# Top-2-of-8 experts on one core: four column groups for gate and up, transposes on the vector engine, a computed one-hot, another order and another end

## The chip, the cores and the metric

The kernel runs on one core of one Trainium2 chip. The metric is the device time of one execution in microseconds (us), and the number that counts is the median of the runs of one kernel. Before the change there were three runs: 1240.44, 1244.74 and 1244.99 us, so the median is 1244.74 us.

The engines are named as in the profile: PE is the matrix engine with its queue of matmuls, PEld its weight loads, DVE the vector engine, ACT the scalar engine, SP the engine that only issues DMA transfers here.

## The reference

The program is a decoder trunk of two residual layers over 256 tokens of 1024 channels, all in float32. Each layer has a token mixer (not touched here) and a channel mixer: a dense SwiGLU in layer 0, and in layer 1 eight SwiGLU experts of which every token uses two:

```
logits = tokens @ router_w                      # 256 x 8
top_val, top_idx = top_k(logits, 2)             # two experts for each token
top_w = softmax(top_val)
out[token] += top_w * ((silu(x_e @ gate[e]) * (x_e @ up[e])) @ down[e])   # for both experts of the token
x = x + out
```

`gate[e]` and `up[e]` are 1024x1792 and `down[e]` is 1792x1024: 22 MB of weights for each expert, 176 MB for the eight, which are all read once from memory in every execution.

## The kernel before, in words

**Stages.** Mixer 0, dense SwiGLU, mixer 1 and then the experts, which take the time from 794 us to the end. Within each engine the instructions run in the order in which the program writes them (`manual_schedule`): no instruction of a queue passes another. What stands between engines is waits on semaphores that the compiler sets for the data.

**Slots.** An expert has 96 places for tokens ("slots", `CAP`), in three blocks of 32 (`CG`). A one-hot matrix `oh` (token by slot, from the rank `pos` of a token within its expert, `onehot`) says which token has which slot. `gather` (L1090s) multiplies the tokens, split in two float32r halves `th` and `tl`, by the one-hot, and so makes `xe`: channels by slots, for two experts at once; each call makes half of the channels (16 matmuls of 192 columns and two copies when nothing was made ahead). The compiled program has the count `n` of tokens of each expert in a register. `rest` (L1104) puts the matmuls of the third block under `If(n > 64)`: on these inputs the third block runs for experts 0, 1, 2 and 4 and is skipped for 3, 5, 6 and 7. A second pass (`more`) for experts with over 96 tokens exists in the program and does not run.

**Weights.** Every weight tile is 128 rows by 1024 columns (512 KB), or 128 by 768 in a second gate/up round (384 KB). SP issues their transfers at L87 (`feed`), in a fixed order, 24 tiles ahead of the tile that PE uses (`RA_MOE`), into 46 places that are also used for the other big buffers (`xe`, `es`, `aT`, `ye`, `ohT`). An issue waits until its place is free. For expert e the order is: gate and up of round 0 (16 tiles), the last six down tiles of expert e-1, gate and up of round 1 (16 tiles), the first eight down tiles of e. PE consumes them in this order.

**One expert.** `gate_up` (L1114) is called twice, for 1024 and for 768 of the 1792 columns. The weights are the moving operand, the slots the stationary one, 32 columns of PE wide, so that four matmuls stand beside each other in the four column groups of PE. Two column blocks (512 or 384 columns, `BN`) by two slot blocks make the four groups: eight matmuls for a pair of gate and up tiles, and after four such pairs those of the third slot block into a bank of its own. A tile's place comes free when the third block's matmuls have read it. Then silu on ACT and products on DVE. `turn` (L1145) transposes the result on PE through two banks (`ps_et`), with one copy on ACT and one on DVE, into `aT`. `down` (L1158) multiplies by the down tiles, four matmuls of 512 columns each, and again the third block after each group of tiles. `scale` (L1177) multiplies the finished rows by the routing weights and splits them in two halves (ACT, then DVE, twice). `back` (L1188) transposes the one-hot with four PE transposes and one ACT copy. `scatter` (L1198) multiplies the transposed one-hot by the rows (16 matmuls), and DVE adds the result to `x`; for the last expert SP then stores each quarter.

**Order.** The loop of `experts` (L1214) interleaves two experts:

```
gate_up(e, 0); down(1) of e-1; scale; back of e-1; turn; [odd e: gather half]
gate_up(e, 1); down(0) of e; turn; [odd e: gather other half]; scatter of e-1
```

At e = 1 `slot_weights` (64 matmuls of two columns, L1084) stands between `down(1)` and `scale`. PE's on-chip accumulators are eight banks of 512 columns, given out in turn.

Of the kernel before, what the change touches and what calls it, by code (L numbers as in the profile page):

```python
# [31 lines left out]
O_ID, O_TU, O_TUS, O_TLS, O_ONE, O_IOTA, O_LT, O_CNT = 0, 128, 256, 384, 512, 640, 768, 832  # L32
O_SLOT = 896
N_CONST = 1152
# [9 lines left out]
BN = (512, 384)  # L44
# [4 lines left out]
class Net:  # L49
# [990 lines left out]
    def moe(self, l, out):  # L1040
# [70 lines left out]
        def group(ps, g, n):  # L1111
            return ps[g * CG:(g + 1) * CG, :n]

        def gate_up(e, i, xe, n):  # L1114
# [3 lines left out]
            if n is not None:  # L1118
                nc.vector.memset(pr[:, :w], 0.0)
            for c in range(2):  # L1120
                ws = []
                for k in range(4 * c, 4 * c + 4):
                    ws.append((self.get_raw(), self.get_raw()))
                    for m, ps in enumerate((pg, pu)):
                        for b in range(2):
                            for s in range(2):
                                mmf(group(ps, 2 * b + s, w), x(k, s), ws[-1][m][:, b * w:(b + 1) * w],  # L1127
                                    start=(k == 0), stop=(k == KD - 1))
                    self.pulse()

                def f():
                    for k in range(4 * c, 4 * c + 4):
                        for m in (1, 0):
                            for b in range(2):
                                mmf(group(pr, 2 * (1 - m) + b, w), x(k, 2), ws[k - 4 * c][m][:, b * w:(b + 1) * w],
                                    start=(k == 0), stop=(k == KD - 1))
                rest(n, f)
            a = self.u("es")
            nc.scalar.activation(a[:, :w], pg[:, :w], AF.Silu)  # L1139
            nc.vector.tensor_mul(a[:, :w], a[:, :w], pu[:, :w])  # L1140
            nc.scalar.activation(a[:64, 512:512 + w], pr[64:, :w], AF.Silu)
            nc.vector.tensor_mul(a[:64, 512:512 + w], a[:64, 512:512 + w], pr[:64, :w])
            return a

        def turn(a, i):  # L1145
            pa, pb = self.ps("et"), self.ps("et")
            at = self.u("aT")[:, :NJ[i] * CAP].rearrange("p (j s) -> p j s", s=CAP)
            n = BN[i] // P
            for c in range(n):
                nc.tensor.transpose(pa[:, c * P:(c + 1) * P], a[:, c * P:(c + 1) * P], self.ident)  # L1150
            for c in range(n):
                nc.tensor.transpose(pb[:, c * 64:(c + 1) * 64], a[:64, 512 + c * P:512 + (c + 1) * P],
                                    self.ident[:64, :64])
            nc.scalar.copy(at[:, :, :64], pa[:, :n * P].rearrange("p (j s) -> p j s", s=64))
            nc.vector.tensor_copy(at[:, :, 64:], pb[:, :n * 64].rearrange("p (j s) -> p j s", s=32))
            return at

        def down(i, at, acc, n):  # L1158
            for c0, c1 in ((0, 4), (4, NJ[i])):
                ws = []  # L1160
                for j in range(c0, c1):
                    ws.append(self.get_raw())
                    for b in range(2):
                        for s in range(2):
                            mmf(group(acc[0], 2 * b + s, 512), at[:, j, s * CG:(s + 1) * CG],  # L1165
                                ws[-1][:, b * 512:(b + 1) * 512], start=(i + j == 0), stop=(i == 1 and j == NJ[1] - 1))
                    self.pulse()

                def f():
                    for j in range(c0, c1):  # L1170
                        for b in range(2):
                            mmf(group(acc[1], 2 * b + j % 2, 512), at[:, j, 2 * CG:], ws[j - c0][:, b * 512:(b + 1) * 512],
# [15 lines left out]
        def back(oh, e):  # L1188
            pt = self.ps("ohT")
            for q in range(2):  # L1190
                for t in range(2):
                    nc.tensor.transpose(pt[:, (2 * q + t) * P:(2 * q + t + 1) * P],  # L1192
                                        self.slots(oh, t, e, q).bitcast(F32), self.ident)
            o = self.u("ohT", F32R)
            nc.scalar.copy(o[:, :512], pt)  # L1195
            return o

        def scatter(y, o, last):  # L1198
            for t in range(2):
                ps = [self.ps("sc"), self.ps("sc")]  # L1200
                for q in range(2):
                    for p in range(2):
                        for b in range(2):
                            r = slice(64 * b, 64 * (b + 1))
                            mmf(ps[b], o[r, (2 * q + t) * P:(2 * q + t + 1) * P], y[q][r, p * 512:(p + 1) * 512],  # L1205
                                start=(q + p == 0), stop=(q + p == 2))
                for b in range(2):
                    h = slice(b * 512, (b + 1) * 512)
                    x = self.x[:, t, h]
                    nc.vector.tensor_add(x, x, ps[b])  # L1210
                    if last:
                        nc.sync.dma_start(out[t * P:(t + 1) * P, h], x)

        def experts(oh, wch, skip):  # L1214
# [3 lines left out]
            acc = y = prev = None  # L1218
            for e in range(NE + 1):
                if e < NE:  # L1220
                    x = xe[e // 2]
                    n = None
                    if skip:
                        n = nc.values_load(self.cni[0:1, e:e + 1], min_val=0, max_val=T, engines=[mybir.EngineType.PE])
# [199 lines left out]
```

## Time and profile before

| | us |
|---|---|
| median of three runs | 1244.74 |
| the profiled execution, its time | 1241.17 |
| its span | 1239.3 |
| PE busy in it | 1203.8 (97%) |
| DVE busy | 640.4 (52%) |
| ACT busy | 442.1 (36%) |

The profile shows one execution. Its span is the time from the first to the last event that the hardware profiler recorded; its own time is 1.9 us longer. Busy time is the time in which an engine had an instruction in work; matmuls overlap, so a row of the timeline that holds eight matmuls gives the time from the start of the first to the end of the last. The granted clock is the share of full speed that PE had (1.00 is 2.4 GHz, 0.50 is 1.2 GHz). A DMA share of 1 means that all 16 DMA engines of the core had packets in work all the time. In the slices of the page, the moved bytes rise from some 150 to 200 GB/s in the first two thirds to over 400 GB/s in the last quarter, which is the experts.

### The profile page before, as it was taken

To read this page: it belongs to the slowest core of one execution; us is meant where nothing else is said; L and a number is where in the kernel's file an instruction comes from. 1 tells how busy PE (TensorE), PEld (TensorE's weight loads), DVE (VectorE), ACT (ScalarE), POOL (GpSimd) and SP (SyncE) were. 2 spreads that over 40 slices of the span, in tenths; PEclk is the share of its full clock that TensorE was granted. 3 is DMA by queue.
4 is the path that set the end of the run, shared out by engine and by line. 5 is a ranking of instruction groups with operands and counts; after the bars stand their busy time and mean duration, and the time that the engine had idled before them with its cause. 6 is when DMAs were issued, how large, how long until landed. Compare 5 with 4: busy or idle time off the path is not lost. (4 is left out here: it accounts for less than half of the span.)

```text
span 1239.3 us, 22611 instructions
## 1 busy us (share of the span) xinstructions
PE 1203.8 (97%) x9536; PEld 885.7 (71%) x9536; DVE 640.4 (52%) x951; ACT 442.1 (36%) x628; POOL 22.7 (2%) x24
## 2 busy tenths in 40 slices
PE   7999999999999999999999999999999999999985
PEld 5899989998899998899989999433433343343322
DVE  6799867686645555789866776510111121112112
ACT  6555555453534543556556442200101011011010
POOL 0100000000000000100000000000000000000000
PEclk9999999999999999999999999899999999999999
DMA  9545444565566564445543569599799999999995
GB/s 367 194 148 188 153 153 136 172 225 216 176 199 198 176 204 174 146 135 171 170 154 122 178 197 348 193 357 373 303 366 349 402 408 403 405 405 399 407 403 205
DMA packets 91122, 312.27 MB, mean 252 GB/s; under 512 B 10240, under 2 KB 10624, under 8 KB 91008
## 3 DMA queue, kind: packets, MB, share of 16 engines
q1 hardware_dynamic: 91008, 310.66, 69.0%
q8 instruction: 83, 1.36, 0.4%
q14 instruction: 31, 0.25, 0.1%
HBM read 309.57 MB, written 1.05 MB: 251 GB/s over the span
## 5 line engine op out<-in xcount | busy, mean ns | idle before, releaser
L100 DVE TENSOR_TENSOR wlo<-raw,whi 128x1024 fp32r<-128x1024 f32 x244 | 289.3, 1218 | 69.3 <-ACT whi L95 61.6
L95 ACT CAST whi<-raw 128x1024 fp32r<-128x1024 f32 x244 | 243.8, 1048 | 19.0 <-DMA raw<-in_w_mix_dram 5.0
L1127 PE MATMUL ps_gg<-raw,xe 128*32 128x384 f32 (+1 forms) x1024 | 121.9, 546 | 2.3 <-PEq L1108 1.4
L1127 PE MATMUL ps_gu<-raw,xe 128*32 128x384 f32 (+1 forms) x1024 | 120.9, 542 | 0.9 <-DMA raw<-in_w_gu_dram 0.4
L1140 DVE TENSOR_TENSOR es<-es,ps_gu 128x512 f32<-128x512 f32 (+1 forms) x16 | 9.9, 621 | 208.1 <-ACT es L1139 171.6
L1165 PE MATMUL ps_ye<-raw,aT 128*32 128x512 f32 x896 | 104.8, 595 | 7.3 <-DMA raw<-in_w_dn_dram 4.6
L157 PE MATMUL ps_gate<-hh,whi 128*128 128x256 f32 x384 | 111.4, 290 | 0.0
L159 PE MATMUL ps_gate<-hl,whi 128*128 128x256 f32 x384 | 108.6, 283 | 0.0
L158 PE MATMUL ps_gate<-hh,wlo 128*128 128x256 f32 x384 | 108.6, 283 | 0.0
L1139 ACT ACTIVATE es<-ps_gg 128x512 f32<-128x512 f32 (+1 forms) x16 | 8.7, 544 | 220.2 <-PE ps_gg L1127 165.9
L1165 PEld LDWEIGHTS ps_ye<-raw,aT 128*32 128x32 f32 x896 | 28.7, 109 | 78.3 <-issue 51.9
L1127 PEld LDWEIGHTS ps_gu<-raw,xe 128*32 128x32 f32 x1024 | 33.7, 110 | 66.0 <-issue 51.9
L1127 PEld LDWEIGHTS ps_gg<-raw,xe 128*32 128x32 f32 x1024 | 31.4, 110 | 64.0 <-issue 49.8
L157 PEld LDWEIGHTS ps_gate<-hh,whi 128*128 128x128 f32 x384 | 73.5, 192 | 0.5
L158 PEld LDWEIGHTS ps_gate<-hh,wlo 128*128 128x128 f32 x384 | 73.5, 191 | 0.5
L159 PEld LDWEIGHTS ps_gate<-hl,whi 128*128 128x128 f32 x384 | 73.5, 191 | 0.0
L157 PE MATMUL ps_xbc<-hh,whi 128*128 128x256 f32 x256 | 73.2, 286 | 0.0
L159 PE MATMUL ps_xbc<-hl,whi 128*128 128x256 f32 x256 | 72.4, 283 | 0.0
L158 PE MATMUL ps_xbc<-hh,wlo 128*128 128x256 f32 x256 | 72.3, 283 | 0.0
L157 PE MATMUL ps_u<-hh,whi 128*128 128x256 f32 x208 | 59.0, 283 | 0.0
L159 PE MATMUL ps_u<-hl,whi 128*128 128x256 f32 x208 | 58.9, 283 | 0.0
L158 PE MATMUL ps_u<-hh,wlo 128*128 128x256 f32 x208 | 58.9, 283 | 0.0
(333 smaller groups left out, 2496.5 us busy)
## 6 DMA issues: line engine op xcount, KB each, us to landing
raw<-in_w_mix_dram SPq DMA_DIRECT2D x178, 512.0 KB, 3.8
raw<-in_w_gu_dram SPq DMA_DIRECT2D x128, 512.0 KB, 10.0
raw<-in_w_dn_dram SPq DMA_DIRECT2D x112, 512.0 KB, 10.0
raw<-in_w_gu_dram SPq DMA_DIRECT2D x128, 384.0 KB, 7.9
raw<-in_w_ffn_dram SPq DMA_DIRECT2D x66, 512.0 KB, 4.4
gain<-in_gains_dram SPq DMA_DIRECT2D x6, 512.0 KB, 4.5
out_dram<-x_res SPq DMA_DIRECT2D x4, 256.0 KB, 3.4
x_res<-in_x_dram SPq DMA_DIRECT2D x2, 256.0 KB, 3.1
```

Source lines behind the costliest of these rows:

```text
L95: nc.scalar.copy(hi, self.raws[self.nhi])
L100: nc.vector.tensor_sub(lo, self.raws.pop(self.nlo), hi.bitcast(F32))
L157: mm(out, lh, rh, start=start, stop=False)
L158: mm(out, ll, rh, start=False, stop=False)
L159: mm(out, lh, rl, start=False, stop=stop)
L1127: mmf(group(ps, 2 * b + s, w), x(k, s), ws[-1][m][:, b * w:(b + 1) * w], start=(k == 0), stop=(k == KD - 1))
L1139: nc.scalar.activation(a[:, :w], pg[:, :w], AF.Silu)
L1140: nc.vector.tensor_mul(a[:, :w], a[:, :w], pu[:, :w])
L1165: mmf(group(acc[0], 2 * b + s, 512), at[:, j, s * CG:(s + 1) * CG], ws[-1][:, b * 512:(b + 1) * 512], start=(i + j == 0), stop=(i == 1 and ...
```

## The change

What it does, part by part:

- **Column groups.** `BN` becomes (256, 192): in `gate_up` the four column groups of PE hold four column blocks of the same slot block, and the slot blocks stand one behind the other in the columns of the accumulator. A tile of gate or up is used by eight matmuls of 256 or 192 columns in place of four of 512 or 384; the third slot block takes four for each tile in place of two of double width.
- **Transposes.** The products then have 32 slots in each group of 32 partitions, and one DVE instruction transposes them in squares of 32 by 32 into `aT`, within `gate_up`. `turn`, with its PE transposes and copies, is gone. The down weights are laid out in memory to fit the new order of rows.
- **One-hot.** `back` no longer transposes the one-hot: DVE makes two diagonal matrices of the positions (`dg`), one PE matmul with a matrix of ones spreads them over all partitions (`pb`, one matmul of 256 columns), and two DVE comparisons with the slot's own number make the transposed one-hot.
- **Order.** Both halves of the next `gather` now come before `gate_up(e, 1)`. The scattering of expert e-1 (`add_back`) comes before `down(0)`, ahead of the clearing of the accumulator `ye` on DVE. It uses four banks; the matmuls of the third slot block are under `If(n > 64)`.
- **End.** For the last expert `back` comes before the first down rows. Before the last down rows four matmuls by the identity load `x` into the four banks; the scattering adds to them, ACT and DVE copy two banks each, and each copy is followed by a store.
- The constants are rearranged to fit.

The core of the diff:

```diff
-BN = (512, 384)
+BN = (256, 192)
...
         def gate_up(e, i, xe, n):
...
-                        for b in range(2):
-                            for s in range(2):
-                                mmf(group(ps, 2 * b + s, w), x(k, s), ws[-1][m][:, b * w:(b + 1) * w],
-                                    start=(k == 0), stop=(k == KD - 1))
+                        for s in range(2):
+                            for b in range(4):
+                                mmf(group(ps, b, s * 256, w), x(k, s), ws[-1][m][:, b * w:(b + 1) * w],
+                                    start=(k + s == 0), stop=(k + s == KD))
...
+            nc.scalar.activation(a2, v(pg), AF.Silu)
+            nc.scalar.activation(a[:, 2 * w:3 * w], pr[:, :w], AF.Silu)
+            nc.vector.tensor_mul(a2, a2, v(pu))
+            nc.vector.tensor_mul(a[:, 2 * w:3 * w], a[:, 2 * w:3 * w], pr[:, 256:256 + w])
+            at = self.u("aT")
+            nc.vector.transpose(at[:, :3 * w], a[:, :3 * w])
+            return lambda j, s: at[:, s * w + j * CG:s * w + (j + 1) * CG]
-        def turn(a, i):
...
-        def back(oh, e):
-            pt = self.ps("ohT")
+        def back(e, pos):
+            dg = self.small("dg", T, F32R)
+            for t in range(2):
+                c = t * NE + e
+                nc.vector.tensor_scalar(dg[:, self.tok(t)], self.ident, pos[:, c:c + 1], None, op0=ALU.mult)
+            pb = self.ps("pb")
+            mmf(pb[:, :T], self.one_r, dg, start=True, stop=True)
+            o = self.u("ohT", F32R)
             for q in range(2):
-                for t in range(2):
-                    nc.tensor.transpose(pt[:, (2 * q + t) * P:(2 * q + t + 1) * P],
-                                        self.slots(oh, t, e, q).bitcast(F32), self.ident)
-            o = self.u("ohT", F32R)
-            nc.scalar.copy(o[:, :512], pt)
+                nc.vector.tensor_scalar(o[:, q * T:(q + 1) * T], pb[:, :T], self.c[:, O_SP + q:O_SP + q + 1], None,
+                                        op0=ALU.is_equal)
             return o
...
+        def scatter(y, o, n, ps, first):
+            def part(q, p, start=False, stop=False):
                 for t in range(2):
+                    for b in range(2):
+                        r = slice(64 * b, 64 * (b + 1))
+                        mmf(ps[t][b], o[r, (2 * q + t) * P:(2 * q + t + 1) * P], y[q][r, p * 512:(p + 1) * 512],
+                            start=start, stop=stop)
+            part(0, 0, start=first)
+            rest(n, lambda: (part(1, 0), part(1, 1)))
+            part(0, 1, stop=True)
+        def add_back(y, o, n):
+            ps = [[self.ps("sc") for _ in range(2)] for _ in range(2)]
+            scatter(y, o, n, ps, True)
+            for t in range(2):
                 for b in range(2):
+                    x = self.x[:, t, b * 512:(b + 1) * 512]
+                    nc.vector.tensor_add(x, x, ps[t][b])
...
         # the loop of experts, after
+            for e in range(NE):
+                at0 = gate_up(e, 0, x, n)
                 if e:
+                    down(1, at1, acc, n0)
                     if e == 1:
                         slot_weights(oh)
                     y = scale(e - 1, acc)
+                    o = back(e - 1, pos)
                 if e % 2 and e < NE - 1:
+                    for q in range(2):
+                        gather(oh, e // 2 + 1, xe[e // 2 + 1], q)
+                at1 = gate_up(e, 1, x, n)
+                if e:
+                    add_back(y, o, n0)
                 acc = [self.ps("ye"), self.ps("ye")]
                 if n is not None:
                     nc.vector.memset(acc[1], 0.0)
+                if e == NE - 1:
+                    o = back(e, pos)
+                down(0, at0, acc, n)
+                n0 = n
+            ps = [[self.ps("sc") for _ in range(2)] for _ in range(2)]
+            h = lambda b: slice(b * 512, (b + 1) * 512)
+            for t in range(2):
+                for b in range(2):
+                    mmf(ps[t][b], self.ident, self.x[:, t, h(b)], start=True, stop=False)
+            down(1, at1, acc, n0)
+            scatter(scale(NE - 1, acc), o, n0, ps, False)
+            for t in range(2):
+                for b in range(2):
+                    (nc.vector.tensor_copy if b else nc.scalar.copy)(self.x[:, t, h(b)], ps[t][b])
+                    nc.sync.dma_start(out[t * P:(t + 1) * P, h(b)], self.x[:, t, h(b)])
```

## Rows read from the trace of the kernel before

Times are us from the start of the span. In an order of work a row holds the start, the duration, the engine and line, what was done (result <- operands, partitions by columns) and the count.

**Rows 1.** Busy time by stage: us, engines, granted clock, DMA share, GB/s

```profile
794.00:961.00 167.00, 166.15 (x1656) 62.27 (x1652) 22.47 (x47) 15.34 (x28) 0.00 (x0) 0.99 0.87 329
961.00:1220.00 259.00, 247.49 (x2346) 92.58 (x2337) 44.58 (x80) 27.00 (x50) 0.00 (x0) 1.00 1.03 404
...
860.00:880.00 20.00, 20.00 (x172) 11.23 (x168) 4.23 (x8) 3.30 (x6) 0.00 (x0) 0.91 0.91 345
```

**Rows 2.** SyncE's waits, 794-961 us: waited for, total us, times, longest

```profile
SPq L87 <- PE ps_gr L1135: 69.7, 16, 13.3
```

**Rows 3.** Order of work, SyncE, 947 to 950 us: start, us, what was issued

```profile
948.19 2.27 SPq L87 DMA_DIRECT2D raw<-in_w_gu_dram  x5
```

**Rows 4.** Order of work, PE, the router: start, us, matmuls

```profile
773.89 0.43 PE L930 MATMUL ps_lg<-hT,wg 128*32 128x128 f32 x8
```

**Rows 5.** Groups by line and shape: count | busy us, mean ns

```profile
L848 PE MATMUL ps_pm<-win,pw 128*128 128x256 f32 x16 | 4.1, 378 | 0.0
L930 PE MATMUL ps_lg<-hT,wg 128*32 128x128 f32 x32 | 1.8, 285 | 0.0
...
L213 DVE CAST cstr<-cst 128x128 fp32r<-128x128 f32 x1 | 0.2, 218 | 0.0
```

**Rows 6.** Order of work, PE, around the end of expert 0's first round

```profile
813.94 0.66 PE L1150 MATMUL ps_et<-cst,es 128*128 128x128 f32 x4
...
815.84 0.85 PE L1127 MATMUL ps_gg<-raw,xe 128*32 128x384 f32 x8
```

**Rows 7.** Order of work, expert 1; then PE after its down rows

```profile
874.62 0.66 PE L1192 MATMUL ps_ohT<-cst,oh 128*128 128x128 f32 x4
...
875.74 1.41 DVE L1183 SCALAR_TENSOR_TENSOR ye<-ps_ye,sw,ye 128x512 fp32r<-128x512 f32 x2 [0.76 <-ACT ye L1182]
...
876.03 0.36 PE L991 MATMUL ps_ga<-oh,th 128*128 128x192 f32 x1
...
879.27 1.15 PE L1127 MATMUL ps_gg<-raw,xe 128*32 128x384 f32 x8
...
905.49 0.55 PE L1150 MATMUL ps_et<-cst,es 128*128 128x128 f32 x3
...
906.29 0.36 PE L991 MATMUL ps_ga<-oh,th 128*128 128x192 f32 x1
...
908.25 2.12 PE L1205 MATMUL ps_sc<-ye,ohT 64*128 64x512 f32 x16
```

**Rows 8.** Order of work, all engines, expert 2

```profile
938.77 0.66 PE L1192 MATMUL ps_ohT<-cst,oh 128*128 128x128 f32 x4
...
939.70 0.75 DVE L1183 SCALAR_TENSOR_TENSOR ye<-ps_ye,sw,ye 128x512 fp32r<-128x512 f32 x1 [0.19 <-ACT ye L1182]
...
940.18 0.85 PE L1127 MATMUL ps_gg<-raw,xe 128*32 128x384 f32 x8
```

**Rows 9.** SyncE's waits, 996 to 1001 us

```profile
SPq L87 <- PEq L1108: 3.7, 1, 3.7
```

**Rows 10.** The DMA view, 961-1220 us: GB/s in 40 slices, issues

```profile
GB/s 408 397 402 399 408 409 409 404 412 402 397 400 408 407 405 412 406 409 397 396 406 407 409 407 407 407 399 395 386 408 405 407 411 407 409 395 397 406 407 388
...
q8 instruction: 24, 0.39, 0.6%
...
raw<-in_w_dn_dram SPq DMA_DIRECT2D x70, 512.0 KB, 10.2
```

**Rows 11.** The DMA view, 800 to 803 us, an issue into an idle queue

```profile
raw<-in_w_dn_dram SPq DMA_DIRECT2D x1, 512.0 KB, 3.9
```

**Rows 12.** Order of work, all engines, the end of the program

```profile
1206.58 0.55 DVE L1140 TENSOR_TENSOR es<-es,ps_gu 128x384 f32<-128x384 f32 x1 [12.73 <-ACT es L1139]
...
1225.13 1.92 PE L1165 MATMUL ps_ye<-raw,aT 128*32 128x512 f32 x16 [0.18 <-PEq L1108]
...
1230.19 2.48 DVE L1210 TENSOR_TENSOR x_res<-x_res,ps_sc 128x512 f32<-128x512 f32 x4 [0.89 <-PE ps_sc L1205]
...
1230.91 2.55 SPq L1212 DMA_DIRECT2D out_dram<-x_res  x4
```

More of the change, by code (lines that the diff above doesn't have):

```diff
@@ L1109, in rest, with group @@
                     f()
[L1111 to L1112 removed]
+        def group(ps, g, o, n):
+            return ps[g * CG:(g + 1) * CG, o:o + n]
         def gate_up(e, i, xe, n):
@@ L1118, in gate_up @@
             if n is not None:
-                nc.vector.memset(pr[:, :w], 0.0)
+                nc.vector.memset(pr, 0.0)
             for c in range(2):
@@ L1132, in f @@
                     for k in range(4 * c, 4 * c + 4):
[L1133 to L1136, printed above, removed]
+                        for m in range(2):
+                            for b in range(4):
+                                mmf(group(pr, b, m * 256, w), x(k, 2), ws[k - 4 * c][m][:, b * w:(b + 1) * w],
+                                    start=(k + m == 0), stop=(k + m == KD))
                 rest(n, f)
             a = self.u("es")
[L1139 to L1143, printed above, removed]
-        def turn(a, i):
[L1146 to L1156, printed above, removed]
+            v = lambda b: b[:, :512].rearrange("p (s c) -> p s c", s=2)[:, :, :w]
+            a2 = a[:, :2 * w].rearrange("p (s c) -> p s c", s=2)
+            nc.scalar.activation(a2, v(pg), AF.Silu)
[5 more added lines that the diff above has]
+            return lambda j, s: at[:, s * w + j * CG:s * w + (j + 1) * CG]
         def down(i, at, acc, n):
@@ L1164, in down @@
                         for s in range(2):
-                            mmf(group(acc[0], 2 * b + s, 512), at[:, j, s * CG:(s + 1) * CG],
-                                ws[-1][:, b * 512:(b + 1) * 512], start=(i + j == 0), stop=(i == 1 and j == NJ[1] - 1))
+                            mmf(group(acc[0], 2 * b + s, 0, 512), at(j, s), ws[-1][:, b * 512:(b + 1) * 512],
+                                start=(i + j == 0), stop=(i == 1 and j == NJ[1] - 1))
                     self.pulse()
@@ L1217, in experts @@
                 gather(oh, 0, xe[0], q)
[L1218 to L1224, printed above, removed]
-                    a0 = gate_up(e, 0, x, n)
+            acc = at1 = n0 = o = None
+            for e in range(NE):
+                x = xe[e // 2]
+                n = None
+                if skip:
+                    n = nc.values_load(self.cni[0:1, e:e + 1], min_val=0, max_val=T, engines=[mybir.EngineType.PE])
+                at0 = gate_up(e, 0, x, n)
                 if e:
-                    down(1, prev[0], acc, prev[1])
+                    down(1, at1, acc, n0)
                     if wch:
@@ L1244, in experts @@
                     nc.vector.memset(acc[1], 0.0)
-                down(0, at, acc, n)
-                prev = turn(a1, 1), n
-                if e % 2 and e < NE - 1:
-                    gather(oh, e // 2 + 1, xe[e // 2 + 1], 1)
-                if e:
-                    scatter(y, o, False)
+                if e == NE - 1:
[13 more added lines that the diff above has]
+                    nc.sync.dma_start(out[t * P:(t + 1) * P, h(b)], self.x[:, t, h(b)])
         self.hold = False
-        experts(self.oh, self.start(weights(self.oh)), SKIP)
+        experts(self.oh, self.pos, self.start(weights(self.oh)), SKIP)
         def more(level):
@@ L1326, in _consts @@
     r = np.arange(1, CAP + 1)
+    c[:, O_SP] = np.tile(r[:64], 2)
+    c[:, O_SP + 1] = np.tile(r[64:], 4)
     c[:, O_SLOT:O_SLOT + SW] = np.concatenate([r[:64], r[:64]] + [r[64:]] * 4)
```

36 lines of the change are left out of this document (7 added, 29 removed).

## The prediction

> **What bounds the kernel now.** I read the page, then busy time by stage, then SyncE's waits, then the order of work on TensorE (PE). The page's chain of waits covers only the last 12 us, so it tells of the end alone; the stages tell the rest. The experts run from 794 us on, in two regimes [rows 1]. From 961 to 1220 us the DMA engines are full (share 1.03, 404 GB/s) and PE's time does not matter. From 794 to 961 us they stand at 0.87, and PE has no gap (166.15 of 167.00 us). There SyncE waits 69.7 us for `ps_gr` matmuls, those of the third slot block [rows 2]: a weight tile's slot is given back only when that block has read it, and no other slot is free. So the end is set by a path: PE from 794 us to the last release that the transfers really waited for, then transfers without a gap, then the tail. The last such release is that at 948.19 us, in the third expert's second gate/up round [rows 3]. PE time saved or lost before it moves the end one for one; later it does so only where PE uses up the queue's reserve, and in the tail.
>
> **The sum, against the profiled run (1241.17 us, span 1239.3).** Experts are counted from 0.
>
> *Twice the matmuls, half the columns: 0.* Sixteen matmuls of 512 columns take 1.92 us with the drain of the last [rows 12], 0.11 us each over four column groups, so a group is busy 0.43 us with one. With 192 columns that is 0.16 us. The nearest row is the router's: eight of 128 columns, with their weight loads, are over in 0.43 us [rows 4], where one lasts 0.285 us [rows 5], so all eight started within 0.145 us, two to a group. Loads and issue keep up with what is asked. Bounds: 0, and rival 3.
>
> *Expert 0: -2.7 us.* PE's transposes go in both rounds: 815.84 - 813.94 = 1.9 us after the first (PE waits there for VectorE) [rows 6], and after the down rows a shorter set, as that of 905.49 to 906.29, 0.8 us [rows 7]. The vector transposes in their place are done long before the down rows that use them: a whole gate/up round of some 15 us lies between. I take 0.9 us for 768 columns: a cast of 128 columns took 0.22 us [rows 5], an addition of 512 took 0.62 [rows 12].
>
> *The new wait.* `back` now begins with two vector operations (a diagonal of positions each), which stand behind `scale` on VectorE. The broadcast matmul needs them, and on PE the gathers and the next gate/up round are queued behind it. Before, PE transposed the one-hot at once.
>
> *Expert 1: +1.1 us.* PE is free at 874.62. The second scale operation ends at 875.74 + 1.41 = 877.15 [rows 7]; two diagonals at 0.22 us (the 128-column cast [rows 5]) and the matmul make 877.9, so 3.3 us. Then come all 32 gather matmuls. The half at 906.29 to 908.25 took 1.96 us; the other, 876.03 to 879.27, took 3.24 us [rows 7], for part of 860 to 880 us ran at the lower clock, 1.2 GHz (granted 0.91 on the mean [rows 1]), after 4 us of two-column matmuls and transposes. After: 3.3 + 3.24 + 1.96 = 8.5 us. Before: 4.65 us from 874.62 and 2.76 us from 905.49, 7.4 us. Bounds -0.2 (both halves at 2.4 GHz) and +2.4 (both at 1.2).
>
> *Expert 2: +1.0 us.* The transposes took 940.18 - 938.77 = 1.41 us. VectorE ends scaling at 939.70 + 0.75 = 940.45 [rows 8]; diagonals and matmul make 941.2, so 2.4 us. Bounds 0 and +2.6 (rival 1). The scatter only moves ahead of the down rows, 2.0 us either way. Its four additions now stand ahead of the clearing of `ye` on VectorE: 0.9 (what VectorE still has of the round's products) + 0.9 (the transposes) + 2.48 + 0.48, about 4.8 us; PE needs the cleared bank after 2.0 + 3.5 us. Covered by 0.7 us; beyond that PE would wait.
>
> At the release of 948.19 us: -2.7 + 1.1 + 1.0 = -0.6 us.
>
> *Expert 3: +0.9 us.* Here SyncE waited 3.7 us for PE [rows 9] and no gap came of it. In this stretch a transfer lands 10.2 us after its issue [rows 10], into an empty queue 3.9 us [rows 11]: the reserve was 10.2 - 3.7 - 3.9 = 2.6 us. Both gather halves now come before the round, which holds one more of the 46 slots (half of the next `xe`) and takes 1.3 us (512 KB at 404 GB/s) of it. PE comes later by 1.0 (the wait) + 1.96 (the gather) - 0.8 (a turn) = 2.2 us, against 1.3 left. Bounds 0 and 2.6. Later odd experts have skipped blocks ahead of them and more reserve.
>
> *Program: +1.2 us.* Instructions come by DMA too: 24 fetches, 0.39 MB, in the full stretch [rows 10]. Some 740 more an expert, at 256 a fetch, are 14 more there: 0.6 us for their bytes. Upper bound: what lies between the best slice (412 GB/s) and the mean (404) [rows 1, 10] is all theirs, 5 us for 24, so 2.9 us. I stay nearer to the bytes.
>
> *Scatter's skip: 0.* Where an expert has at most 64 tokens, eight matmuls (1.0 us) go and a branch comes. These experts (3, 5, 6, 7) lie where transfers bind.
>
> *Tail: +0.5 us.* The last `back` stands behind two products, a transpose, four additions, a clearing and two diagonals on VectorE: from 1206.58 [rows 12] 1.1 + 0.9 + 2.48 + 0.48 + 0.44 us, so 1212.0, with its matmul 1212.3. Then PE has 14 down tiles of eight matmuls (112 x 0.107 = 12.0 us), three skipped blocks at 0.2 to 0.4 us, and the four matmuls that load x into PSUM: float32 on the full array, in columns the same as sixteen of 256 that took 4.1 us [rows 5]. 1212.3 + 12.0 + 1.0 + 4.1 = 1229.4, against 1225.13 + 1.92 = 1227.05 now [rows 12]: +2.4. From there to the issue of the last store it is 1230.91 + 2.55 - 1227.05 = 6.4 us now; after: one scaling on both engines 1.55, half the scatter 0.55, two copies on each of two engines 1.4, the stores on their heels 0.9: 4.4, so -2.0. Bounds -1.5 (PE catches up with the transfers) and +2.4 (the new end saves nothing).
>
> Sum: -0.6 + 0.9 + 1.2 + 0.5 = +2.0 us, so 1243.2 us on the profiled run's scale. That run lies 3.6 us under the median of the three (1244.74), which makes 1246.7 us by the median.
>
> **Rivals.** 1. *The clock falls at the new waits.* For it: the fall near 876 us after little PE work. Against: the 1.4 us of transposes in the other experts caused none (1.00 in 961 to 1220 us [rows 1]). Price: a gather half in 3.24 instead of 1.96 us and a slow start of the round, some 1.6 us each time. With 1.3 more in expert 1, 1.6 in expert 2 and 1.6 in expert 3 it is +4.5: 1251. From a fall in each of these three on, the kernel is slower.
> 2. *The wait is no wait:* VectorE makes the diagonals while it waits for ScalarE. Then expert 1 gives -2.0 us, expert 2 -1.2, expert 3 costs nothing and the tail gives -1.5; with -2.7 and +0.8 it is -6.6: 1238.
> The Trainium skill, "TensorE: Matmul & The Clock Gate", section "Architectural detail", says that VectorE's queue is strictly first in, first out. By that rule the diagonals cannot pass the scaling, and this rival falls. The trace agrees as far as it goes: the row at 939.70 stands right behind its wait for ScalarE, with nothing between [rows 8].
> 3. *A matmul costs as such, not by its columns.* If one of 256 columns took the 0.1 us of one of 512, the 256 more an expert would be 26 us, and 13 in the four experts with a third block: 8 x 26 + 4 x 13 = 260 us, with PE the bound, 1490. For it: no row has 192 or 256 columns in column groups. Against it: the router's row [rows 4].
> The same page, section "Back-to-back issue gap", gives some 81 ns for each matmul of 128 columns in a stream with weight loads and 131 ns for 512. By that rule (an estimate: 95 ns at 256 columns) this rival would hold. The trace disagrees: 0.11 us at 512, and eight of 128 columns started within 0.145 us [rows 4, 12].
> 4. *Fetches cost more* than the slices show, 0.6 us each through the transfers they hold up: +7 on top, 1254.
>
> **Chances.** Forecast 0.62, rival 1 0.16, rival 2 0.13, rival 3 0.03, rival 4 0.06. The measurement tells 0.5%, 6.2 us, from no change: under 1238.5 is faster, over 1250.9 slower. The forecast's own range, from the bounds taken together in moderation, is 1242 to 1251; rival 2 below and rivals 1 and 4 above make it 1239.5 to 1253. Faster: rival 2 and a little of the forecast, 0.15. Slower: rivals 3 and 4, half of rival 1 and a little of the forecast, 0.21. Same: 0.64.
>
> **What would show it.** Right: no `et` and `ohT` transposes on PE; expert 0's second round follows its first at once; from expert 1 on PE stands 2 to 3.3 us before a `pb` matmul, released by VectorE; eight 256-column matmuls take 0.43 us; DMA share 1.03 from about 961 us on; in the tail PE some 4 us behind the transfers, and copies on two engines ahead of the stores. Wrong: the share under 1 after 1010 us; the clock under 1 in experts 2 and 3; 256-column matmuls over 60 ns each; the last weight tile landing more than 4 us from where it landed.

## The result: 1.8% slower, and where the time lies in the profile after

| | before | after |
|---|---|---|
| median, us | 1244.03 (5 runs) | 1264.77 (5 runs) |
| ratio | | 1.018, 95% interval 1.0163 to 1.0197 |
| span of the profiled execution, us | 1239.3 | 1264.8 |

The forecast was 1246.7 us with a range up to 1253; the measured time lies 12 us above that range. First the stages of the changed kernel, in the columns of [rows 1]; the last row is a piece of the tail.

```profile
794.00:961.00 167.00, 161.85 (x2704) 105.99 (x2698) 25.45 (x52) 10.65 (x21) 0.00 (x0) 0.95 0.83 326
961.00:1220.00 259.00, 231.07 (x3489) 136.07 (x3488) 53.27 (x98) 16.81 (x33) 0.00 (x0) 0.98 1.01 404
...
1226.00:1252.00 26.00, 21.74 (x176) 7.57 (x165) 5.67 (x12) 0.82 (x2) 0.00 (x0) 0.87 0.00 1
```

Read the last row first. From 1226 to 1252 us the DMA engines move nothing, and PE still has 21.74 us of matmuls: all weights are on the chip, about as early as before, and PE comes over 26 us behind them. Its last down rows end at 1250.57 + 1.92 = 1252.49 us; before they ended at 1227.05 [rows 12]. These rows and the issue of the stores, changed kernel:

```profile
1250.57 1.92 PE L1155 MATMUL ps_ye<-raw,aT 128*32 128x512 f32 x16 [0.18 <-PEq L1107]
...
1255.30 3.29 SPq L1255 DMA_DIRECT2D out_dram<-x_res  x4
```

So in the changed kernel PE is the bound to the end. In 961 to 1220 us it stands still for 28 us (259.00 - 231.07); before for 11.5 [rows 1].

PE's waits from 794 us on (engine, what waits, for whom: us in total, times, longest), changed kernel:

```profile
PE ps_pb L1185 <- DVE dg L1183: 20.1, 8, 3.3
PE ps_ye L1155 <- PEq L1107: 5.0, 10, 2.0
PE ps_sc L1197 <- PEq L1107: 4.2, 6, 2.9
PE ps_gg L1126 <- issue: 2.7, 3, 1.6
PE ps_gg L1126 <- PEq L1107: 2.0, 6, 1.1
PE ps_gg L1126 <- DMA raw<-in_w_gu_dram: 1.5, 4, 1.0
PE ps_gu L1126 <- issue: 1.4, 1, 1.4
```

The part of the first of them in 961 to 1220 us, and then the waits of the kernel before in that stretch:

```profile
PE ps_pb L1185 <- DVE dg L1183: 11.9, 5, 2.7
```

```profile
PE ps_ye L1165 <- DMA raw<-in_w_dn_dram: 4.6, 13, 1.8
PE ps_ye L1165 <- PEq L1108: 2.0, 10, 0.3
PE ps_gg L1127 <- PEq L1108: 1.4, 8, 0.2
PE ps_gg L1127 <- DMA raw<-in_w_gu_dram: 0.7, 4, 0.2
PE ps_et L1150 <- PEq L1108: 0.7, 4, 0.2
PE ps_ohT L1192 <- PEq L1108: 0.5, 3, 0.2
PE ps_ye L1165 <- DMA raw<-in_w_gu_dram: 0.4, 1, 0.4
PE ps_gu L1127 <- DMA raw<-in_w_gu_dram: 0.4, 2, 0.2
```

Before, PE's longest waits were for weights. After, they are two new things. One is the wait for the diagonals, 20.1 us in all eight experts. The other, with `PEq` (PE's own sequencer, at the line of the If) and `issue` as the releaser, is PE standing still at an If or behind it, for no data that the profile shows: single gaps of up to 2.9 us, where before none was over 0.3. What PE lacks in these gaps is taken up with the column part.

The wait in expert 2, all engines (weight loads and SP left out), in the columns of [rows 8]:

```profile
940.87 1.64 DVE L1173 SCALAR_TENSOR_TENSOR ye<-ps_ye,sw,ye 128x512 fp32r<-128x512 f32 x2 [5.74 <-ACT ye L1172]
...
942.41 0.47 DVE L1183 TENSOR_SCALAR dg<-cst,pos 128x128 fp32r<-128x128 f32 x2
942.94 0.38 PE L1185 MATMUL ps_pb<-dg,cstr 128*128 128x256 f32 x1 [2.01 <-DVE dg L1183]
943.26 0.86 PE L1126 MATMUL ps_gg<-raw,xe 128*32 128x192 f32 x16
```

The diagonals start only when both scalings are done, although VectorE had stood idle for 5.74 us before these and the diagonals need nothing of them: VectorE worked its queue off in the order of the program. The last row shows the doubled matmuls: 16 of 192 columns last 0.86 us with the drain, as eight of 384 did (0.85 us, [rows 6]). (In gate/up and down rounds the profile shows two rows for each matmul of the program.)

### The profile page after: what moved, and what is told of

Same layout as the page of the kernel before. It is cut to its first block, busy times and chain, and to the rows that moved or that the text cites. A ratio compares the mean times of both kernels' runs of the same rounds, so it can differ in the third digit from the quotient of the medians.

```text
span 1264.8 us, 27421 instructions
## 1 busy us (share of the span) xinstructions
PE 1201.3 (95%) x11936; PEld 981.0 (78%) x11936; DVE 654.6 (52%) x981; ACT 428.8 (34%) x606; POOL 22.7 (2%) x24
## 5 line engine op out<-in xcount | busy, mean ns | idle before, releaser
L1126 PE MATMUL ps_gg<-raw,xe 128*32 128x192 f32 (+1 forms) x2048 | 129.8, 362 | 7.3 <-issue 2.7
L1126 PE MATMUL ps_gu<-raw,xe 128*32 128x192 f32 (+1 forms) x2048 | 129.4, 359 | 1.4 <-issue 1.4
L1126 PEld LDWEIGHTS ps_gg<-raw,xe 128*32 128x32 f32 x2048 | 72.6, 112 | 41.8 <-issue 14.8
L1126 PEld LDWEIGHTS ps_gu<-raw,xe 128*32 128x32 f32 x2048 | 74.9, 112 | 29.1 <-issue 3.0
L1155 PEld LDWEIGHTS ps_ye<-raw,aT 128*32 128x32 f32 x896 | 33.1, 111 | 68.4 <-issue 58.0
```

What stands on the lines that cost most here:

```text
L1126: mmf(group(ps, b, s * 256, w), x(k, s), ws[-1][m][:, b * w:(b + 1) * w], start=(k + s == 0), stop=(k + s == KD))
L1155: mmf(group(acc[0], 2 * b + s, 0, 512), at(j, s), ws[-1][:, b * 512:(b + 1) * 512], start=(i + j == 0), stop=(i == 1 and j == NJ[1] - 1))
```

## The experiments

Each is against the kernel before on the same chip, as a ratio with its 95% interval. An expectation was written before its run.

### Taking the wait away, and putting it alone into the kernel before

Diagonals ahead (`e1_diag_ahead`; for the last expert they stand ahead of `add_back`):

```diff
                 at0 = gate_up(e, 0, x, n)
                 if e:
+                    dg = diag(e - 1, pos)      # the two tensor_scalar of back
                     down(1, at1, acc, n0)
...
-                    o = back(e - 1, pos)
+                    o = back(dg)
```

> Changed kernel with one move: the two diagonals of positions are made on VectorE ahead of the scaling, so that the broadcast matmul has them when PE arrives. Theory A (PE's 20.1 us of waits for the diagonals, and the lower clock after them, are the loss; PE became the bound): the eight pb waits fall under 0.5 us each, the clock stays at 1.00 after 890 us, PE catches up with the transfers again and the time is 1238 to 1245 us. Rival B (the loss is in PE's instruction stream, twice the matmuls and longer jumps): only the waits themselves come back, PE stays behind the transfers to the end, 1246 to 1252 us.

Measured: 1243.73 us, 1.0005 (0.9989 to 1.0021). The waits are gone (0.3 us left) and with them 21 us. But PE did not catch up: the stalls stay, and this row of 1216 to 1230 us has the transfers done (0.01) and PE busy:

```profile
1216.00:1230.00 14.00, 12.81 (x88) 4.00 (x88) 0.00 (x0) 0.46 (x1) 0.00 (x0) 1.00 0.01 1
```

The time is as theory A has it, the reason half of it.

The new one-hot alone in the kernel before, first with its wait (`e4_before_new_back`: `back`, its constants and its arguments from the change), then with the diagonals ahead (`e12_before_diag_ahead`: the diff above on top). Both also have the constants of the change, whose own part is measured further down:

> Kernel before with one part of the change: only the one-hot by diagonals, broadcast and comparisons in place of the four PE transposes (constants rearranged for it). Theory A: eight waits of 2 to 3 us come on PE and the lower clock after most of them; the transposes' 8 x 0.49 us go; PE's slack before the end (11.5 us in 961 to 1220 us) is used up: 1250 to 1258 us. Rival C (in the stretch in which the transfers are full, PE's time does not matter, as the prediction had it): 1243 to 1247 us.

> Kernel before with the new one-hot alone, its diagonals made ahead of the scaling. Theory A (it was the wait, not the broadcast and the comparisons): PE saves the transposes' 8 x 0.49 us and waits nowhere: 1240 to 1243.5 us. Rival H (the other VectorE operations or the matmul of ones cost as much as the transposes and more): 1246 us or more.

Measured: 1258.64 us, 1.0127 (1.0097 to 1.0157) with the wait; 1230.67 us, 0.9906 (0.9886 to 0.9926) without it, the fastest kernel of this study, faster than the kernel before and than the changed one. So eight waits of 19.6 us in the trace cost 0.0221 of 1244 = 27.5 us. Rival C, which was the prediction's own view of this stretch, falls. The stages 961 to 1220 us, with the wait and then without it:

```profile
961.00:1220.00 259.00, 242.64 (x2228) 94.88 (x2223) 50.41 (x98) 24.17 (x43) 0.00 (x0) 0.95 0.98 391
```

```profile
961.00:1220.00 259.00, 249.82 (x2390) 97.74 (x2382) 56.08 (x112) 26.08 (x47) 0.00 (x0) 1.00 0.99 399
```

With the wait the granted clock is 0.95 on the mean, without it 1.00: a wait costs itself and slower matmuls behind it. The lateness also reaches the transfers. Their GB/s in 40 slices of 961 to 1220 us (6.5 us each), with the wait, then in the changed kernel:

```profile
GB/s 412 417 413 417 416 417 420 139 365 411 418 412 413 420 407 419 224 254 412 417 414 412 418 422 415 186 358 419 414 413 416 416 419 417 416 416 418 412 414 418
```

```profile
GB/s 408 416 413 416 416 417 361 121 401 417 413 412 415 416 419 416 417 418 414 416 411 414 420 417 383 400 393 410 415 415 414 419 418 416 416 413 411 415 417 417
```

In the kernel before no slice is under 386 [rows 10]. The three dips with the wait alone, and the one of the changed kernel at about 1006 to 1013 us, come behind waits of PE; SP then waits 9.5 to 9.7 us at a time (10.5 in the changed kernel), and for PE, which gives the places back late. So the stretch in which the transfers were full is no longer full.

That the clock falls because PE stands still was tried by filling the wait with spare work (`e7_filled_wait`):

```diff
             pb = self.ps("pb")
+            for _ in range(8):
+                mmf(pb[:, :T], self.ident, self.x[:, 0, :T], start=True, stop=True)
```

> Changed kernel with eight spare matmuls (identity by 256 columns of x, about 2 us) on PE ahead of each broadcast matmul, so that PE works where it waited. Theory A (the clock falls because PE stands still for 2 to 3 us): the granted clock stays at 1.00 behind the waits of experts 2, 3 and 6 and at the last back, and though work was added the time falls by 4 to 9 us to 1256 to 1261 us. Rival D (the clock falls for another reason, the waits cost only themselves): the falls stay, time 1264 to 1268 us.

Measured: 1270.81 us, 1.0234 (1.0206 to 1.0261). The stretch behind the wait of expert 2, changed kernel, then filled:

```profile
943.00:961.00 18.00, 18.00 (x387) 13.69 (x389) 1.92 (x4) 0.68 (x2) 0.00 (x0) 0.91 0.89 339
```

```profile
943.00:961.00 18.00, 18.00 (x406) 14.00 (x408) 3.32 (x7) 0.82 (x2) 0.00 (x0) 1.00 0.89 344
```

The clock stays up, so the fall does come of standing still, and rival D is out. Over the 9 us behind each of the eight waits the clock is under 1.00 five times in the changed kernel, seven times in e4 and never in the filled one. But not every wait brings it down. Behind this one of 2.00 us, changed kernel, it stayed:

```profile
1108.71:1117.71 9.00, 9.00 (x161) 7.82 (x161) 2.47 (x5) 0.96 (x2) 0.00 (x0) 1.00 1.03 417
```

Which waits bring it down is not shown. My number was wrong: the eight matmuls run as 16 rows of 0.21 us, 3.4 us instead of 2, so that filling costs more than it brings.

### The column part

In the kernel before (`e5_before_columns`: `gate_up`, `down` and the weights' layout of the change, `turn` gone), undone in the changed kernel (`e11_old_columns`), undone with the diagonals ahead (`e8_diag_ahead_old_columns`), and added to the fastest kernel (`e16_ahead_columns`):

> Kernel before with one part of the change: four column blocks, 32x32 transposes on VectorE and the relaid down weights; back, order and end as before. Theory S (doubled matmuls are free while they flow, but where a third block is skipped PE then stands still for instructions, 13 us in all in experts 3, 5, 6, 7): the PE transposes' 16 us go, stalls of 0.8 to 3 us come only in the experts with a skipped block, none in 0, 1, 2, 4; 1238 to 1245 us. Rival B (a doubled number of matmuls costs everywhere): 1248 us or more.

> Changed kernel with the column part alone undone (diagonals where the change has them, so that PE's eight waits stay). Theory A (waits and instruction stalls are two losses on one engine that add up): 7.8 us less than the changed kernel, 1255 to 1259 us. Rival G (without the stalls PE has the slack to hide the waits): under 1250 us.

> Diagonals ahead, and the column part undone: two column blocks by two slot blocks, PE transposes and copies as before; order, one-hot and end of the change kept. Theory S: the stalls of 0.8 to 3 us at skipped blocks go to 0.2 to 0.4 us, the PE transposes' 16 us come back: 1238 to 1246 us. Rival F (the stalls come of the scatter's If and of the order, not of the number of matmuls): they stay and the transposes come on top: 1255 us or more.

> Kernel before with the new one-hot made ahead (1230.7 us) and the column part on top. Theory S (the stalls at skipped blocks, 13 to 18 us, eat the 16 us of transposes that go, and come late, where nothing can be caught up): 1231 to 1238 us, with the stalls in experts 3, 5, 6, 7 alone. Rival U (without waits the column part is a gain): under 1229 us.

| kernel | with the columns | without them |
|---|---|---|
| before | 1246.96 us, 1.0039 (1.0024 to 1.0055) | 1 |
| new one-hot ahead, on before | 1242.17 us, 1.0004 (0.9992 to 1.0015) | 1230.67 us, 0.9906 |
| changed, diagonals ahead | 1243.73 us, 1.0005 | 1235.94 us, 0.9942 (0.9925 to 0.9960) |
| changed | 1264.77 us, 1.0180 | 1264.60 us, 1.0168 (1.0146 to 1.0191) |

In the three kernels without the diagonals' waits the columns cost 4 to 10 of 1000, 5 to 12 us; my theory S (stalls and saved transposes cancel) had the stalls right and the sum wrong, and all four times lie outside the ranges that I gave. Rivals F, G and U fall; of B little remains, for most of the loss is at skipped blocks (the bill below). In the changed kernel undoing the columns gave nothing clear (the expected 7.8 us didn't come). The traces show why the two losses do not add up: from 794 us on, `PEq` and `issue` gaps are 23.9 us with the diagonals ahead and 15.9 in the changed kernel, and 6.8 and 6.6 without the columns. With the waits there, some 8 us of the gaps are not; how a wait takes them in is not shown. PE's waits in the fastest kernel with the columns:

```profile
PE ps_ye L1155 <- PEq L1107: 5.4, 13, 1.7
PE ps_gg L1126 <- issue: 4.1, 3, 2.5
PE ps_gg L1126 <- PEq L1107: 3.5, 7, 1.7
PE ps_ye L1155 <- issue: 3.0, 2, 1.6
PE ps_gu L1126 <- issue: 2.8, 4, 1.8
```

Without the columns the same kernel has 5.4 us of PEq waits in all (3.2, 0.8, 0.7 and 0.7), none over 0.3. The bill, from the starts of PE's rounds in the two traces: gate/up rounds 269.1 against 248.5 us, of it 16 in the eight rounds with a skipped third block and 5 in the eight others; down rows 134.2 against 129.0; transposes 0 against 13.8. That is +20.6 + 5.2 - 13.8 = 12.0 us. One of the stalls, and what it does to the matmuls behind it (expert 7):

```profile
1202.45 0.85 PE L1126 MATMUL ps_gg<-raw,xe 128*32 128x192 f32 x14
1205.82 0.35 PE L1126 MATMUL ps_gg<-raw,xe 128*32 128x192 f32 x1 [2.51 <-issue]
...
1207.18 1.47 PE L1126 MATMUL ps_gg<-raw,xe 128*32 128x192 f32 x12
...
1209.64 0.81 PE L1126 MATMUL ps_gg<-raw,xe 128*32 128x192 f32 x12
```

Twelve matmuls take 1.47 us at 1207.18 us, where the granted clock is 0.50, and 0.81 at 1209.64, where it is 1.00: behind the stall PE runs at the lower clock at first.

What does PE wait for in these gaps? Three tries. Shorter jumps (`e3_four_ifs`):

```diff
-            for c in range(2):
+            for c in range(4):
                 ws = []
-                for k in range(4 * c, 4 * c + 4):
+                for k in range(2 * c, 2 * c + 2):
```

> Changed kernel; the third block's matmuls of a gate/up round stand under four Ifs of 16 instead of two of 32, so that a skipped block is a shorter jump. Theory B1 (PE stands still for instructions because the jump over a skipped block leaves what was fetched): the gaps of 0.8 to 2.9 us at skipped blocks and behind them, 13.6 us in all, fall under 5 us, time 1254 to 1259 us. Rival B2 (it is the number of instructions per us that the fetches cannot follow, not the jump): the gaps stay, time 1263 to 1268 us.

Measured: 1275.15 us, 1.0272 (1.0235 to 1.0310). Stalls of the same size are there, in part at other places, and twice the Ifs add some 0.17 us or more each. Both B1 and B2 miss.

No jumps in the gate/up rounds, on the fastest kernel with the columns (`e18_columns_no_skip`: `f()` for `rest(n, f)` there):

> New one-hot made ahead and the column part (1242.2 us), but the third block of the gate/up rounds runs for every expert, without an If (the result is the same; it adds about 64 matmuls a round where it was skipped, some 41 us of PE in all). Theory J (PE stands still for instructions behind a jump): gaps of over 0.6 us within and right behind gate/up rounds, ten in the run with the Ifs, are gone; the time is some 25 to 30 us longer. Rival I (instructions cannot be brought as fast as the doubled matmuls use them up): the gaps stay.

Measured: 1269.7 us, 1.0220 (1.0189 to 1.0251, from two runs), as theory J has the time. PE's waits:

```profile
PE ps_gr L1134 <- issue: 2.6, 4, 1.3
...
PE ps_gu L1126 <- issue: 1.7, 1, 1.7
PE ps_ye L1155 <- PEq L1107: 1.0, 6, 0.2
```

Ten gaps of over 0.6 us ahead of the last scatter fall to three, and the PEq waits before down rows from 5.4 to 1.0 us. So most of it hangs on the jump, but three `issue` gaps of up to 1.7 us stay without one: both theories hold in part. That the doubled code is fetched too late is the likeliest reading, and the traces support it. They record the fetches: 16 KB each, on the queue q8 of [rows 10]. This one lies between 1203 and 1204 us, as the gap shown above begins:

```profile
q8 instruction: 1, 0.02, 5.9%
```

By the times of these records, each of the ten gaps of e16 ends 1.3 to 1.8 us after a fetch has landed, and each of the three of e18 1.3 to 1.5 us after one, though fetches mostly come 6 us or more apart. What holds such a fetch up behind a jump is not shown.

The count of the next expert loaded earlier (`e9_diag_early_counts`, on diagonals ahead, `values_load` within the first down rows):

> Diagonals ahead, and the count of the next expert's tokens is loaded into PE's register within the first down rows, with 12 matmuls behind which it can hide, instead of right behind the skipped block at the head of the next expert. Theory R (the three gaps of 1.0 to 1.1 us ahead of experts 4, 6 and 7 are this load): they fall to 0.2 to 0.4 us, 1240.5 to 1242.5 us. Rival S2 (they are instruction fetches after the jump like the others): the gaps stay, 1243 to 1245 us.

Measured: 1244.72 us, 1.0016 (1.0004 to 1.0028). The three gaps of 1.0 to 1.1 us are gone from the trace, as theory R has it, but the time is not less. In the profiled executions PE's last scatter ends 2.0 us earlier (1229.95 us against 1231.90), but from there to the end of the span it takes 1.8 us longer (11.7 against 9.9); why is open.

### The end

Old end on diagonals ahead (`e6_diag_ahead_old_end`), and on diagonals ahead with old columns (`e10_diag_columns_end`):

```diff
-            for t in range(2):
-                for b in range(2):
-                    mmf(ps[t][b], self.ident, self.x[:, t, h(b)], start=True, stop=False)
             down(1, at1, acc, n0)
-            scatter(scale(NE - 1, acc), o, n0, ps, False)
+            scatter(scale(NE - 1, acc), o, n0, ps, True)
...
-                    (nc.vector.tensor_copy if b else nc.scalar.copy)(self.x[:, t, h(b)], ps[t][b])
+                    nc.vector.tensor_add(self.x[:, t, h(b)], self.x[:, t, h(b)], ps[t][b])
```

> Diagonals ahead (as the first run) and, beside it, the end of before: no matmuls that load x into PSUM, the scatter starts the banks and VectorE adds them to x ahead of each store. Theory P (PE is the bound up to the last down rows): 3.6 us of PE go, two more VectorE operations of 0.62 us come behind the scatter: 1240 to 1242.5 us. Rival E (the transfers are the bound there and the new end is worth 2 us, as the prediction had it): 1245 to 1247 us.

> Diagonals ahead, old columns and old end together: what is left of the change is the one-hot by broadcast, the gathers and the scatter moved forward and the scatter's If. Theory P (PE is still the bound up to the last down rows): the 3.6 us of PE for loading x go, 1.2 us of VectorE come: 1232 to 1234 us. Rival T (with the stalls gone the transfers are the bound at the end): 1235 to 1237 us.

Measured: 1239.50 us, 0.9974 (0.9957 to 0.9991), against 1.0005 with the new end; and 1233.86 us, 0.9913 (0.9895 to 0.9932), against 0.9942. The new end costs some 3.7 us each time: theory P. For the last expert's broadcast ahead of its last down rows in the fastest kernel (`e17_ahead_last_back`):

> Kernel before with the new one-hot made ahead (1230.7 us), and for the last expert the broadcast and the comparisons ahead of its last down rows. Theory A: the wait of 2.05 us before the last scatter goes: 1228 to 1229.5 us. Rival: the end is set by the scaling and the stores, which come no earlier: 1230 to 1231.5 us.

Measured: 1234.66 us, 0.9937 (0.9913 to 0.9961) against 0.9906, no gain, and above both ranges. The wait of 2.05 us before the scatter is gone, but the same 2.1 us now stand before the earlier broadcast.

### A part of the change that no one named: where the buffers lie

The fastest kernel gained more than its waits and transposes explain, and in its trace the transfers move 416 GB/s in 1060 to 1160 us, before 403. The trimmed constants move the 46 buffers from byte 38880 of each partition (480 past a multiple of 512) to a multiple of 512. The constants alone in the kernel before (`e13_before_trimmed`), the old offset in the fastest (`e14_ahead_shifted`) and in the changed kernel (`e15_after_shifted`):

```diff
-O_ID, ..., O_IOTA, O_LT, O_CNT = 0, 128, 256, 384, 512, 640, 768, 832
-N_CONST = 1152
+O_ID, ..., O_LT, O_CNT, O_SLOT, O_SP = 0, 128, 256, 384, 512, 640, 704, 768, 1024
+N_CONST = 1026
...
+        pad = self.cp.tile([P, 120], F32, tag="pad", name="pad")     # e14, e15 alone
```

> Kernel before with only the constants rearranged as in the change (126 columns fewer), which moves the 46 buffers of 4096 bytes to an address that is a multiple of 512 bytes in each partition (38400; before 38880). No instruction differs. Theory M (where the buffers lie sets the rate of the transfers): a 512 KB tile lands every 1.24 us, and as the transfers are the bound from 961 to 1220 us, the time is 1234 to 1239 us. Rival N (the rate comes of the new one-hot, with fewer reads of on-chip memory by PE and ScalarE): 1.28 us and 1242 to 1246 us.

> Kernel before with the new one-hot made ahead, and an unused buffer of 480 bytes ahead of the 46, so that they start at 40928, 480 bytes past a multiple of 512, as in the kernel before. Theory M: 1.28 us for a tile, and the time goes from 1230.7 back to 1238 to 1242 us. Rival N: 1.24 us and 1229 to 1233 us.

> Changed kernel with the same unused buffer of 480 bytes. Theory M with PE as the bound: tiles land every 1.28 us, later by up to 8 us at the end, and the time stays within 3 us of the changed kernel's (1262 to 1268 us), for PE comes 20 us behind the transfers. Rival Q (the faster transfers did help the changed kernel): 1269 us or more.

Measured: 1236.12 us, 0.9955 (0.9941 to 0.9969); 1239.74 us, 0.9977 (0.9962 to 0.9991); 1270.72 us, 1.0228 (1.0212 to 1.0244). What the transfers moved in 1060 to 1160 us, kernel before, constants trimmed, and fastest kernel with the offset put back:

```profile
DMA packets 12194, 40.33 MB, mean 403 GB/s; under 512 B 1355, under 2 KB 1355, under 8 KB 12183
```

```profile
DMA packets 12554, 41.65 MB, mean 417 GB/s; under 512 B 1393, under 2 KB 1393, under 8 KB 12543
```

```profile
DMA packets 12152, 40.18 MB, mean 402 GB/s; under 512 B 1351, under 2 KB 1351, under 8 KB 12141
```

But for the load of the constants at the start no instruction differs between the first two: the offset makes 14 GB/s, and 6 us where the transfers are the bound. (Rival N falls. In the fastest kernel the offset makes 8.8 us, good to some 3.) It helped the changed kernel too, by 6 us, so rival Q holds: I had thought that a kernel with PE as its bound would not feel it. With the offset put back PE stands still for 43.6 us from 794 us on, without it for 40.0. The difference is in `PEq` and `issue` gaps (19.6 against 15.9 us), not in waits for weights; by which path the slower transfers lengthen these is not settled.

## Why the prediction was wrong, step by step

The parts, undone in one order (ratios times 1244 us; each step is good to 2 to 3 us, and the sum comes out by construction):

| step | us |
|---|---|
| constants trimmed: buffers on a multiple of 512 bytes | -5.6 |
| new one-hot, diagonals ahead | -6.1 |
| gathers and scatter moved, scatter's If, last `back` early | +0.9 |
| new end | +3.6 |
| columns and vector transposes | +7.8 |
| diagonals behind the scaling | +21.8 |
| sum | +22.4 |

The order matters for the last two: with the columns undone first, they come to 1.5 us and the diagonals to 28.1. The step of +0.9 is not clear of zero.

- **The step that failed: "From 961 to 1220 us ... PE's time does not matter."** Besides the tail the prediction made one exception, "where PE uses up the queue's reserve", and worked it out in expert 3 alone; in experts 4 to 7 it charged the wait at nothing because the transfers were the bound. But PE had little to spare. Of its 11.5 us of standing still in 259 [rows 1], 6.1 were waits for weights, and 4.6 were the `PEq` gaps, which stay. In the changed kernel the same stretch has 11.9 us of waits for the diagonals and 12.9 of `PEq` and `issue` gaps, and the bound changes sides. e4 and e12 show it for the wait without the columns, the order and the end.
- **How PE fell behind.** The wait itself was priced well where it was priced: 3.3 us in expert 1 (3.3 measured, 2.9 of it waiting), 2.4 in expert 2 (2.3, from 940.93 to 943.26 us, 2.0 of it waiting). It is there in experts 3 to 7 as well, 2.0 to 2.7 us each time, and 3.25 at the end, 20.1 us in all. The sum of -0.6 us at the release of 948.19 us was wrong all the same: PE starts that round at 943.26 us, 3.1 us later than before (940.18 [rows 8]). The second round of expert 3 and the first of expert 7, before:

```profile
994.54 0.85 PE L1127 MATMUL ps_gg<-raw,xe 128*32 128x384 f32 x8
...
1167.65 1.07 PE L1127 MATMUL ps_gg<-raw,xe 128*32 128x512 f32 x8
```

And after:

```profile
1003.24 0.86 PE L1126 MATMUL ps_gg<-raw,xe 128*32 128x192 f32 x16
...
1191.18 1.07 PE L1126 MATMUL ps_gg<-raw,xe 128*32 128x256 f32 x16 [1.10 <-PEq L1107]
```

That is 8.7 and 23.5 us late, and 25.4 at the last down rows. Expert 3, priced at 0.9 us, cost the transfers some 5 (an estimate from the two low slices above). Of the four signs of being wrong two came: the clock under 1 in experts 2 and 3, and the transfers not full after 1010 us.

- **The clock (rival 1)** was the right mechanism with its place drawn too small. I expected up to three falls at 1.6 us each by 1000 us; in e4 the clock is at 0.95 over the whole of 961 to 1220 us. In expert 1 both gather halves ran at the lower clock, 6.9 us (875.54 to 882.45) where the sum had 5.2.
- **Columns at 0.** Right while the matmuls flow: steps of 16 with 256 columns follow each other in 0.86 us, and 16 with 192 in 0.65, as eight with 384 did. The 81 to 131 ns a matmul that the Trainium skill gives in "TensorE: Matmul & The Clock Gate", section "Back-to-back issue gap", don't hold here: it is 54 ns at 256 columns in four column groups, so rival 3 falls. What was missed are PE's gaps at skipped blocks: 16 us in the rounds with one (e16). The scatter's If, priced at 0, has 4.2 us of such gaps in the changed kernel. The prediction had counted the fetches well (14 more in the full stretch; 36 instead of 24 were measured) and charged them to the transfers (+1.2 us, rival 4), not to PE.
- **Expert 0: -2.7.** Right: the first gate/up round of expert 1 starts 842.56 - 839.70 = 2.9 us earlier, 0.4 of it from an earlier start.
- **Rival 2** (the diagonals pass the scaling) fell as forecast. Made possible by hand, in e1, it is worth 21.8 us; I had put 8.6 between it and the forecast.
- **Tail: +0.5.** The loading of x was priced at 4.1 us and the saving at 2.0; the matmuls took 3.7, and e6 and e10 show 3.7 us of loss, so the saving did not come: from the last down rows to the issue of the last store it takes 1255.30 + 3.29 - 1252.49 = 6.1 us, before 6.4, forecast 4.4.
- **Not in the sum at all:** the constants line. I read it as bookkeeping; it was worth -5.6 us and hid a fifth of the loss. That the weights were all on the chip about when they were before looked like a confirmed forecast and was two errors of opposite sign: faster transfers, and the stop in expert 3.

## What to carry to other kernels

When one resource is full and another 96% busy, a part that adds work or a wait to the second is not free: write down how long it waits for the full one as its reserve and charge every recurrence against it, to the end of the program. An operation that needs nothing of those ahead of it in its engine's queue belongs ahead of them; two instructions moved up a few lines were worth 22 to 28 us here. And a change that shifts where buffers lie is a change of its own; compare transfer rates before telling a story about the rest.

## What the runs showed of the hardware

- The 4096-byte-per-partition transfers into on-chip buffers ran at 417 GB/s where these start on a multiple of 512 bytes and at 403 where they start 480 bytes past one (e13, e14). Only these two offsets were tried.
- PE standing still for 2 to 3 us was followed by the lower clock in five of eight waits of the changed kernel and seven of eight in e4, and in none of the eight with PE kept busy (e7); a PE stall of 2.5 us at a skipped block did the same (clock 0.50, expert 7 above).
- With twice the matmuls between the same transfers, PE stood still for 0.7 to 2.5 us, ten times with jumps over skipped blocks (e16) and three times without them (e18); halving the jump did not help (e3). Each of these thirteen gaps ended 1.3 to 1.8 us after an instruction fetch of 16 KB had landed; why the fetch came late is open.
